# A decoder layer in split float32: the sums of a pair of down-projection blocks given one by one, a plain row block moved ahead of the second pair, and the up units split in one piece

## The chip, the cores and the metric

The kernel runs on one core of a Trainium2 chip. The core has five engines with a queue each: PE (TensorE, matmuls, with PEld for its weight loads), DVE (VectorE), ACT (ScalarE), POOL (GpSimd) and SP (SyncE, which here issues most DMAs). Each works through its own queue in order, and they wait for each other by semaphores. The metric is the device time of one execution in microseconds (us), lower being better. Before the change it is 417.64 us, the median of three runs (417.42 to 418.87).

## What is computed

One layer of a hybrid decoder, 256 tokens of 1024 channels, in float32. The change touches only the feed-forward part, the last third of the time:

```python
x = layer_norm(ALPHA * x + merged @ w_out[i], ln1_g[i], ln1_b[i])
h = jnp.square(jax.nn.relu(x @ w_up[i])) @ w_down[i]
ple = jax.nn.sigmoid(x @ w_ple_gate[i]) * (p[i] @ w_ple[i])
x = layer_norm(ALPHA * x + h + ple, ln2_g[i], ln2_b[i])
```

`w_up` is 1024 x 4096 and `w_down` 4096 x 1024.

## The kernel before

**Split operands.** PE takes float32 operands in a rounded form (F32R). To keep precision, each operand is split in a high part, rounded, and a low part, the rest. A product is three matmuls: high by high, high by low, low by high (`prod`, line 183). A weight unit is one [128, 1024] block. `Weights._split` gives its instructions: the DMA into `raw` (L102, from SP), the high part `whi` on ACT (L111, or L109 where the block is cut), and the low part `wlo` = raw - whi on DVE (L118, or L122). `whi` and `wlo` have five buffers each, so a unit's ACT instruction waits until PE has finished the unit five places back. `W.get(u)` returns a unit and gives out splits up to four units ahead (AHEAD). `W.subs` lists the last low-part instruction of every unit given so far.

**Up product.** 32 units, `f` from 0 to 31 (L922 on). Each takes eight 512-column matmuls with whi (L932) and eight 256-column ones with wlo (L935); DVE then sums the result out of PSUM (L916), ACT applies relu and square (L917, L918), and the result is split in turn. With the table `UP` (L639) the 128-column blocks of whi and wlo don't lie in one run: block 0 stands apart from the other seven (whi at 16 and then 192 to 1088, wlo at 64 and then 208 to 1104). The class `Apart` turns that into two instructions for each part, 256 and 768 columns wide in the profile.

**Down product.** The 32 row blocks of `w_down` are taken in the order of `SEQ` (L860), then 26 to 31 (`LATE`). A plain row block is one unit and 12 matmuls of 512 columns. A *pair* of row blocks is multiplied by a scheme of the Strassen kind: seven products of half blocks, 21 matmuls, for four units. For those, sums of the weights are formed on DVE first. `load(i)` fetches the two row blocks of pair i, three DMAs on SP (L885, L887 twice), into the buffer `xr` (two in turn). `form(i)` makes three sums: L894, 1024 wide, into `rows` (odd pairs) or `Y` (even); L895, 512 wide, into the loaded block itself; L896, 512 wide. The pair's units are then, in order: the second row block as loaded (unit 0), the first sum (unit 1), the first row block with the second sum in it (unit 2), the third sum, 512 wide (unit 3). Unit 0's raw is the loaded block; L118 rows read `wlo<-xr`, `wlo<-rows` or `wlo<-Y` for a pair's units and `wlo<-raw` for a plain block.

**What sets the order.** A scheduler with priorities places instructions on each engine's queue, by and large in the order in which the program gives them. Pair 0, blocks (0, 1), is loaded and formed in the up loop. Pairs 1 and 2, (4, 5) and (8, 9), are loaded and formed before the down product starts (L964). From then on, when unit 3 of pair i has been split, `last_part` puts pair i + 2 on the list `later`, and `weights` loads and forms it at once, all three sums in a row. The accumulators are the PSUM banks `P[1]` to `P[8]`; behind the last pair, `plus` (L1006) adds them up on DVE while PE multiplies blocks 24 and 25.

Of the kernel before, what the change touches and what calls it, by code (L numbers as in the profile page):

```python
# [13 lines left out]
ALU = mybir.AluOpType  # L14
# [128 lines left out]
def hybrid_layer(ctx: ExitStack, tc: tile.TileContext, x0, xn, pT, wqk, wva, wvb, wg, wbc, wba,  # L143
                 wout, wup, wdn, wpg, wple, lnrow, rel, onehot, pick, out):
    nc = tc.nc
    pe, act, dve, pool = nc.tensor, nc.scalar, nc.vector, nc.gpsimd
# [9 lines left out]
    W = Weights(tc, raw, part)  # L156
# [20 lines left out]
    t = banks.tile([128, 512], F32, name="b4", tag="b4")  # L177
# [54 lines left out]
    def add(*a, at=(0, 0), by=DV):  # L232
        i = n_u[0]
        n_u[0] += 1
        return W.add(*a, by=by if i < 58 else "v", at=at)
# [12 lines left out]
    for t in TASKS:  # L248
# [4 lines left out]
        elif t in "gcao":  # L253
            u, w, n = {"g": (u_g, wg, 1024), "c": (u_bc, wbc, 640), "a": (u_ba, wba, 768),
                       "o": (u_out, wout, 1024)}[t]
# [31 lines left out]
    def mmbank(shape):  # L287
        t = mm.tile([128, 512], F32, name="mm", tag="mm")
        return t[:, 0:256] if shape == 256 else t
# [89 lines left out]
    op = pm.tile([128, 8, 2, S], F32R, name="op")  # L379
# [159 lines left out]
    for j in range(4):  # L539
        s = s[2:] if j % 2 else logits(kI, iq[j], iq[j + 1])  # L540
        r = wk2.tile([128, 768], F32, name="ri", tag="eb")
        r = r.rearrange("p (h k) -> p h k", h=2)
        for h in range(2):
            act.activation(r[:, h], s[h], AF.Relu)
            n = 2 * j + h
# [42 lines left out]
    for j in range(3):  # L588
# [5 lines left out]
        for h in range(2):  # L594
            n = 2 * j + h
# [10 lines left out]
    for j in range(3):  # L606
        s = logits(kA, q)
        o = opair()
        for h in range(2):
            n = 2 * j + h  # L610
# [3 lines left out]
            with tc.issue_after(W.subs[-3]):  # L614
                pool.tensor_tensor(ta[:, 0:128], natural(T, n % 3, 128, 256), am[:, 0:128],
                                   op=ALU.add)
                pool.tensor_tensor(ta[:, 128:384], natural(T, n % 3, 0, 256), am[:, 128:384],
                                   op=ALU.add)
# [17 lines left out]
    u_out += [add(wout[4 + i], 1024, wo[:, i, 0], wo[:, i, 1]) for i in range(4)]  # L636
    u_ple = [add(wple[i], 1024) for i in range(2)]
    u_pg = [add(wpg[i], 1024) for i in range(8)]
    UP = (16, *range(192, 1088, 128)), (64, *range(208, 1104, 128))  # L639
    u_up = [[add(wup[i], 1024, at=UP)] for i in range(32)]  # L640

    H = (slice(0, 512), slice(512, 1024))
# [152 lines left out]
    for i in range(4):  # L795
# [4 lines left out]
        t = slice(b * 128, (b + 1) * 128)  # L800
# [51 lines left out]
    for b in range(2):  # L852
        for c in range(2):
# [3 lines left out]

    SEQ = ((0, 1), 2, 3, (4, 5), 6, 7, (8, 9), 10, (11, 12), 13, (14, 15), 16, (17, 18), 19,  # L860
           (20, 21), 22, 23, 24, 25)
    LATE = range(26, 32)
    PAIRS = [k for k in SEQ if isinstance(k, tuple)]
    hT, at, room = {}, 0, 0
    for k in (*SEQ, *LATE):
        i = PAIRS.index(k) if k in PAIRS else -1
        n = 512 if i < 0 else 1792
        if i in (0, 1):
            t = p2.tile([128, 2048], F32R, name=("X", "PL")[i], tag=("X", "PL")[i])[:, 0:n]
        elif i in (2, 3) or k == 2:  # L870
            t = more[:, room:room + n]
            room += n
        else:
            t = store[:, at:at + n]
# [4 lines left out]
    wr, wt = {}, {}  # L879

    def load(i):

        wr[i] = r = xr[:, i % 2] if i else p3.tile([128, 2, D], F32, name="rows", tag="rows")
        k1, k2 = PAIRS[i]
        nc.sync.dma_start(r[:, 0], wdn[k1])  # L885
        for h in range(2):
            nc.sync.dma_start(r[:, 1, H[h]], wdn[k2, :, H[1 - h]])  # L887

    def form(i):

        t = p3.tile([128, 2, D], F32, name="rows", tag="rows") if i % 2 else Y
        wt[i] = t = t.rearrange("p b d -> p (b d)")
        r = wr[i].rearrange("p b d -> p (b d)")
        dve.tensor_tensor(t[:, 0:1024], r[:, 512:1536], r[:, 0:1024], op=ALU.subtract)  # L894
        dve.tensor_tensor(r[:, 512:1024], r[:, 1024:1536], t[:, 0:512], op=ALU.subtract)  # L895
        dve.tensor_tensor(t[:, 1024:1536], r[:, 1536:2048], r[:, 512:1024], op=ALU.subtract)  # L896

    def last_part(i):
        r = wt[i][:, 1024:1536]
        if 0 < i < len(PAIRS) - 2:  # L900
            later.append(i + 2)
        return r

    later = []
    u_dn = {}
    for k in (*SEQ, *LATE):
        if k in PAIRS:
            i = PAIRS.index(k)
            u_dn[k] = [add(f, n) for f, n in (
                (lambda i=i: wr[i][:, 1], 1024), (lambda i=i: wt[i][:, 0:1024], 1024),  # L910
                (lambda i=i: wr[i][:, 0], 1024), (lambda i=i: last_part(i), 512))]
        elif k < 30:
            u_dn[k] = [add(wdn[k], 1024)]

    def relu2(dst, ps):
        dve.tensor_reduce(dst, ps.rearrange("p a t b -> p b t a"), axis=AX.X, op=ALU.add)  # L916
        act.activation(dst, dst, AF.Relu)  # L917
        act.activation(dst, dst, AF.Square)  # L918
# [3 lines left out]
    for f in range(32):  # L922
        if f == 16:
            with tc.issue_after(W.loads[-1]):
                load(0)
            with tc.issue_after(W.subs[-1]):
                form(0)
        ps = mmbank(512).rearrange("p (a t b) -> p a t b", a=2, b=2)
        hi, lo = W.get(u_up[f][0])
        cs = [slice(k * 128, (k + 1) * 128) for k in range(KT)]  # L930
        for k, c in enumerate(cs):
            pe.matmul(ps, lhsT=hi[:, c], rhs=x1[:, :, k].rearrange("p b a t -> p a t b"),  # L932
                      start=k == 0, stop=False)
        for k, c in enumerate(cs):
            pe.matmul(ps[:, 0], lhsT=lo[:, c], rhs=x1[:, :, k, 0].rearrange("p b t -> p t b"),  # L935
                      start=False, stop=k == KT - 1)
        if f not in half_of:
            spare = f % 2 == 0
            q = (p3.tile([128, 2, 128], F32, name="q1", tag="q1") if spare else
                 w2.tile([128, 8, 128], F32, name="a8", tag="a8")[:, 0:2])  # L940
            relu2(q, ps)
            q = q.rearrange("p b t -> p (b t)")
            act.copy(hT[f][:, 0], q)
            dve.tensor_tensor(hT[f][:, 1], q, hT[f][:, 0].bitcast(F32), op=ALU.subtract)
            continue
        j = half_of[f].index(f)
        if j == 0:
            a8 = w2.tile([128, 8, 128], F32, name="a8", tag="a8")
        relu2(a8[:, 2 * j:2 * j + 2], ps)
        if j == 0:  # L950
            continue

        a21, a11, a22, a12, *sums = (a8[:, j] for j in range(8))
        pool.tensor_tensor(sums[0], a21, a22, op=ALU.add)
        pool.tensor_tensor(sums[1], sums[0], a11, op=ALU.subtract)
        pool.tensor_tensor(sums[2], a11, a21, op=ALU.subtract)  # L956
        pool.tensor_tensor(sums[3], a12, sums[1], op=ALU.subtract)
        h = hT[half_of[f]]
        q = a8[:, 1:8].rearrange("p j t -> p (j t)")
        act.copy(h[:, 0], q)  # L960
        dve.tensor_tensor(h[:, 1], q, h[:, 0].bitcast(F32), op=ALU.subtract)

    xr = p3.tile([128, 2, 2, D], F32, name="xr", tag="x1")
    for i in (1, 2):  # L964
        load(i)
        form(i)

# [6 lines left out]
        fresh.discard(i)  # L976

    def weights(u):
        w = W.get(u)
        while later:  # L980
            i = later.pop(0)
            load(i)
            form(i)
        return w

    def plain(k, w, ids, end=False):
# [6 lines left out]
    TERMS = ((2, 2, 1), (3, 6, 0)), ((7, 5, 1), (5, 3, 0)), ((1, 0, 0), (6, 4, 1)), ((4, 1, 0),)  # L993
    for k in SEQ[:-2]:
        if k not in PAIRS:
            plain(k, weights(u_dn[k][0]), (3, 2, 4, 8), k == 23)
            continue
        for u, terms in zip(u_dn[k], TERMS):
            hi, lo = weights(u)
            for i, a, c in terms:  # L1000
                a = slice(128 * a, 128 * a + 128)
                onto(i, (hT[k][:, 0, a], hT[k][:, 1, a]), (wide(hi, H[c]), wide(lo, H[c])),
                     k == PAIRS[-1] and i in (1, 5, 6, 7))
# [56 lines left out]
    for b in range(2):  # L1060
        t = slice(128 * b, 128 * b + 128)
# [114 lines left out]
```

## Time and profile before

| | |
|---|---|
| three runs, us | 417.42, 417.64, 418.87 |
| the profiled execution, us | 417.59 |
| its span, first to last instruction, us | 415.8 |
| PE busy, us (share of the span) | 404.6 (97%) |
| PEld busy | 374.1 (90%) |
| DVE busy | 348.3 (84%) |
| ACT busy | 277.4 (67%) |
| POOL busy | 121.6 (29%) |
| DMA, GB/s mean over the span | 201 |

Times in rows of the profile are microseconds from the span's start, unless marked ns. A row of the timeline gives start, duration, engine, line, operation, what is written and read, and how many such instructions are merged; a bracket behind it gives the idle time of the engine before it and what ended it. PE's matmuls are pipelined: the next starts while the last one is still under way, so its busy share says little, and the distance between starts is what counts. A tile's name stands without its number (`b` and `mm` are PSUM banks, `store`, `more`, `X` and `PL` hold the split activations).

### The profile page before, as it was taken

Reading aid. Unit: us, or ns where it says so; the run is one execution under the profiler, and the core shown is the slowest. Engines: PE = TensorE matmul, PEld = TensorE weight load, DVE = VectorE, ACT = ScalarE, POOL = GpSimd, SP = SyncE. Lnnn points to the kernel's source line nnn. Section 1 sums busy time; section 2 is a strip of 40 time slices with the busy share of each in tenths; the row PEclk is TensorE's granted clock in tenths of the full one; section 3 lists DMA queues with packets and bytes.
Section 4 is the critical chain, followed back from the end, with each engine's and each line's share of the span. In section 5 each row is a group of like instructions: output and inputs, shape, how many; then the busy total and the mean of one; then the engine's idle time right before and its main releaser. Section 6 shows DMA issues by size and latency. Waiting matters only on the chain.

```text
span 415.8 us, 7826 instructions
## 1 busy us (share of the span) xinstructions
PE 404.6 (97%) x2804; PEld 374.1 (90%) x2804; DVE 348.3 (84%) x650; ACT 277.4 (67%) x530; POOL 121.6 (29%) x128
## 2 busy tenths in 40 slices
PE   8999999999999999999999999999999999899993
PEld 7989999999999999999887889999999888688882
DVE  4868769897777789889978889999999797999856
ACT  5787476495798786867515668887889675558310
POOL 1579456175353657500000002433330000000001
PEclk9999999999999999999999999999999999999998
DMA  8796766567474408477981677695675377546502
GB/s 283 291 338 184 273 166 199 170 202 259 143 208 135 134 18 285 123 217 259 332 314 36 225 268 207 223 298 177 195 214 186 128 271 215 189 159 212 192 2 102
DMA packets 27964, 83.49 MB, mean 201 GB/s; under 512 B 3184, under 2 KB 6792, under 8 KB 27540
## 3 DMA queue, kind: packets, MB, share of 16 engines
q1 hardware_dynamic: 27360, 81.51, 60.3%
q10 hardware_dynamic: 468, 1.41, 0.9%
q8 instruction: 22, 0.36, 0.4%
q14 instruction: 18, 0.15, 0.1%
q0 software_dynamic: 96, 0.06, 0.0%
HBM read 81.88 MB, written 1.09 MB: 200 GB/s over the span
## 4 chain that ended last, share of the span: by engine, by line
PE 79%; DVE 9%; DMA 6%; ACT 2%; issue 2%; SPq 0%; POOL 0%; DVEq 0%; ACTq 0%
PE mm L188 34%; PE b L188 17%; PE mm L932 13%; PE mm L935 7%; DMA xr<-in_wdn_dram 3%; PE b L370 3%; DVE wlo L118 3%; PE b L522 2%; DVE wlo L122 2%; DMA G<-in_x_dram 1%; DMA pr<-in_pT_dram 1%; PE b L412 1%; ACT whi L111 1%; PE b L419 1%; DVE Y L894 1%
## 5 line engine op out<-in xcount | busy, mean ns | idle before, releaser
L111 ACT CAST whi<-raw 128x1024 fp32r<-128x1024 f32 (+3 forms) x92 | 89.5, 986 | 35.6 <-PE b L188 14.5
L122 DVE TENSOR_TENSOR wlo<-raw,whi 128x256 fp32r<-128x256 f32 (+3 forms) x118 | 94.7, 826 | 15.3 <-ACT whi L111 11.4
L188 PE MATMUL mm<-xh,whi 128*128 128x256 f32 x336 | 89.1, 278 | 0.0
L122 POOL TENSOR_TENSOR wlo<-raw,whi 128x384 fp32r<-128x384 f32 (+1 forms) x50 | 68.7, 1383 | 65.0 <-ACT whi L111 57.6
L188 PE MATMUL mm<-xl,whi 128*128 128x256 f32 x336 | 87.1, 277 | 0.0
L188 PE MATMUL mm<-xh,wlo 128*128 128x256 f32 x336 | 79.4, 278 | 0.0
L188 PEld LDWEIGHTS mm<-xh,whi 128*128 128x128 f32 x336 | 64.5, 192 | 0.9
L188 PEld LDWEIGHTS mm<-xl,whi 128*128 128x128 f32 x336 | 64.5, 192 | 0.2
L932 PE MATMUL mm<-x,whi 128*128 128x512 f32 x256 | 60.8, 380 | 0.0
L188 PEld LDWEIGHTS mm<-xh,wlo 128*128 128x128 f32 x336 | 58.7, 192 | 0.2
L188 PE MATMUL b<-whi,store 128*128 128x512 f32 x168 | 52.5, 380 | 0.3 <-DVE b L1006 0.3
L932 PEld LDWEIGHTS mm<-x,whi 128*128 128x128 f32 x256 | 46.1, 190 | 5.1
L118 DVE TENSOR_TENSOR wlo<-raw,whi 128x1024 fp32r<-128x1024 f32 (+2 forms) x38 | 43.2, 1156 | 3.5 <-ACT whi L111 3.4
L749 POOL TENSOR_TENSOR rs<-rs,half 128x1 f32<-128x1 f32 x4 | 2.7, 666 | 142.5 <-DVE rs L748 142.5
L109 ACT CAST whi<-raw 128x256 fp32r<-128x256 f32 x64 | 36.4, 613 | 6.1 <-PE b L188 3.7
L188 PEld LDWEIGHTS b<-whi,store 128*128 128x128 f32 x168 | 31.8, 189 | 4.9 <-DVE b L1006 0.7
L935 PEld LDWEIGHTS mm<-x,wlo 128*128 128x128 f32 x256 | 33.6, 191 | 1.7
L935 PE MATMUL mm<-x,wlo 128*128 128x256 f32 x256 | 33.8, 275 | 0.0
L188 PE MATMUL b<-wlo,store 128*128 128x512 f32 x84 | 32.1, 382 | 0.6 <-DVE wlo L118 0.6
L956 POOL TENSOR_TENSOR a<-a 128x128 f32<-128x128 f32 x7 | 7.3, 1042 | 57.3 <-ACT a L918 51.7
L188 PE MATMUL mm<-op,whi 128*128 128x256 f32 x128 | 22.1, 278 | 0.0
L188 PE MATMUL b<-whi,x 128*128 128x512 f32 x64 | 19.8, 384 | 0.1
(221 smaller groups left out, 818.9 us busy)
## 6 DMA issues: line engine op xcount, KB each, us to landing
raw<-in_wup_dram SPq DMA_DIRECT2D x32, 512.0 KB, 4.4
raw<-in_wg_dram SPq DMA_DIRECT2D x24, 512.0 KB, 4.6
raw<-in_wqk_dram SPq DMA_DIRECT2D x18, 512.0 KB, 5.0
raw<-in_wdn_dram SPq DMA_DIRECT2D x18, 512.0 KB, 4.3
raw<-in_wout_dram SPq DMA_DIRECT2D x8, 512.0 KB, 4.5
raw<-in_wpg_dram SPq DMA_DIRECT2D x8, 512.0 KB, 5.2
T<-tabd SPq DMA_DIRECT2D x24, 128.0 KB, 4.0
xr<-in_wdn_dram SPq DMA_DIRECT2D x6, 512.0 KB, 3.6
```

What stands on the lines that cost most here:

```text
L109: i = nc.scalar.copy(blocks(hi, a, b), blocks(r, a, b))
L111: i = nc.scalar.copy(hi, r)
L118: i = e.tensor_tensor(lo[:, x], r[:, x], hi[:, x].bitcast(F32), op=ALU.subtract)
L122: i = e.tensor_tensor(blocks(lo, *x), blocks(r, *x), blocks(hi, *x).bitcast(F32), op=ALU.subtract)
L188: i = pe.matmul(ps, lhsT=a[x], rhs=b[y], start=first and n == 0, stop=last and n == 2, skip_group_check=more)
L370: m = pe.matmul(ss[2 * n + h][:, QC[b]], lhsT=q[d, x, c], rhs=k[d, y, 0:128 * (b + 1)], start=i == 0, stop=i == 2)
L412: pe.transpose(t[:, 128 * i:128 * i + 128], P[:, 128 * i:128 * i + 128], ident)
L419: pe.matmul(v[:, 256 * i:].rearrange("p (m c q) -> p m c q", c=64, q=2), lhsT=V[:, i, vh], rhs=pt[:, b0:b1].rearrange("p b a (q c) -> p (b ...
L522: pe.matmul(pairs(first[f]), lhsT=w[:, k, 128 * f:128 * f + 128], rhs=inturn(x[:, k]), start=k == i == 0, stop=k == KT - 1 and i == 2)
L932: pe.matmul(ps, lhsT=hi[:, c], rhs=x1[:, :, k].rearrange("p b a t -> p a t b"), start=k == 0, stop=False)
L935: pe.matmul(ps[:, 0], lhsT=lo[:, c], rhs=x1[:, :, k, 0].rearrange("p b t -> p t b"), start=False, stop=k == KT - 1)
L956: pool.tensor_tensor(sums[2], a11, a21, op=ALU.subtract)
```

## The change

There are three edits. The up units lie in one run, whi from column 64 and wlo from 80, so that each part is one instruction; blocks 1 to 7 stay at their columns, and block 0 moves (whi from 16 to 64, wlo from 64 to 80). Plain block 6 comes ahead of the pair (4, 5). And `form` becomes a generator that gives one sum at each call: the three sums of pair i are given behind the splits of units 1, 2 and 3 of pair i - 1, those of pair 1 behind the plain blocks 2, 3 and 6, each after that unit's last low-part instruction. Pair 0 and the loads are given as before.

```diff
-    UP = (16, *range(192, 1088, 128)), (64, *range(208, 1104, 128))
+    UP = 64, 80
...
-    SEQ = ((0, 1), 2, 3, (4, 5), 6, 7, (8, 9), 10, (11, 12), 13, (14, 15), 16, (17, 18), 19,
+    SEQ = ((0, 1), 2, 3, 6, (4, 5), 7, (8, 9), 10, (11, 12), 13, (14, 15), 16, (17, 18), 19,
...
-        dve.tensor_tensor(t[:, 0:1024], r[:, 512:1536], r[:, 0:1024], op=ALU.subtract)
-        dve.tensor_tensor(r[:, 512:1024], r[:, 1024:1536], t[:, 0:512], op=ALU.subtract)
-        dve.tensor_tensor(t[:, 1024:1536], r[:, 1536:2048], r[:, 512:1024], op=ALU.subtract)
+        yield dve.tensor_tensor(t[:, 0:1024], r[:, 512:1536], r[:, 0:1024], op=ALU.subtract)
+        yield dve.tensor_tensor(r[:, 512:1024], r[:, 1024:1536], t[:, 0:512], op=ALU.subtract)
+        yield dve.tensor_tensor(t[:, 1024:1536], r[:, 1536:2048], r[:, 512:1024],
+                                op=ALU.subtract)
...
+    for i in range(1, len(PAIRS)):
+        behind = u_dn[PAIRS[i - 1]][1:] if i > 1 else u_dn[2] + u_dn[3] + u_dn[6]
+        for n, u in enumerate(behind):
+            steps[u] = i, n
+    going = {}
...
     for i in (1, 2):
         load(i)
-        form(i)
...
     def weights(u):
+        n = W.done
         w = W.get(u)
         while later:
-            i = later.pop(0)
-            load(i)
-            form(i)
+            load(later.pop(0))
+        for n in range(n, W.done):
+            if n in steps:
+                with tc.issue_after(W.subs[n]):
+                    next(going.setdefault(steps[n][0], form(steps[n][0])))
         return w
```

How that moves DVE's queue is seen at three places. First, between plain block 10 and plain block 13, where pair 3, (11, 12), is split and pair 4, (14, 15), is formed. Pair 3's sums lie in `rows`, pair 4's in `Y`. Before:

```order
L118 TENSOR_TENSOR wlo<-raw,whi 128x1024
L894 TENSOR_TENSOR Y<-xr 128x1024
L118 TENSOR_TENSOR wlo<-xr,whi 128x1024
L118 TENSOR_TENSOR wlo<-rows,whi 128x1024
L895 TENSOR_TENSOR xr<-xr,Y 128x512
L118 TENSOR_TENSOR wlo<-xr,whi 128x1024
L118 TENSOR_TENSOR wlo<-rows,whi 128x512
L896 TENSOR_TENSOR Y<-xr 128x512
L118 TENSOR_TENSOR wlo<-raw,whi 128x1024
```

and now:

```order
L118 TENSOR_TENSOR wlo<-raw,whi 128x1024
L896 TENSOR_TENSOR rows<-xr 128x512
L118 TENSOR_TENSOR wlo<-xr,whi 128x1024
L118 TENSOR_TENSOR wlo<-rows,whi 128x1024
L894 TENSOR_TENSOR Y<-xr 128x1024
L118 TENSOR_TENSOR wlo<-xr,whi 128x1024
L118 TENSOR_TENSOR wlo<-rows,whi 128x512
L895 TENSOR_TENSOR xr<-xr,Y 128x512
L118 TENSOR_TENSOR wlo<-raw,whi 128x1024
L896 TENSOR_TENSOR Y<-xr 128x512
```

Pair 4's first sum stood ahead of all four splits of pair 3 and now stands behind two of them; its second sum moves behind the other two, and its third behind plain block 13.

Second, DVE's first sums of the down product, pairs 1 and 2 (pair 1 in `rows`, pair 2 in `Y`). Before:

```order
L894 TENSOR_TENSOR rows<-xr 128x1024
L118 TENSOR_TENSOR wlo<-xr,whi 128x1024
L895 TENSOR_TENSOR xr<-xr,rows 128x512
L894 TENSOR_TENSOR Y<-xr 128x1024
L118 TENSOR_TENSOR wlo<-rows,whi 128x1024
```

and now:

```order
L894 TENSOR_TENSOR rows<-xr 128x1024
L118 TENSOR_TENSOR wlo<-raw,whi 128x1024
L118 TENSOR_TENSOR wlo<-xr,whi 128x1024
L895 TENSOR_TENSOR xr<-xr,rows 128x512
L118 TENSOR_TENSOR wlo<-rows,whi 128x1024
L894 TENSOR_TENSOR Y<-xr 128x1024
```

The split of plain block 6 now stands between pair 1's first sum and its first split, and pair 2's first sum moves behind pair 1's unit 1.

Third, DVE in the up loop, behind the split of the activations of pair 0. Before:

```order
L961 TENSOR_TENSOR X<-a_3543,X 128x896
L944 TENSOR_TENSOR more<-q_3606,more 128x256
L122 TENSOR_TENSOR wlo<-raw,whi 128x2x128
L122 TENSOR_TENSOR wlo<-raw,whi 128x768
L916 TENSOR_REDUCE a_3668<-mm 128x256
```

and now (the same code stands five or six lines further down in the changed file):

```order
L967 TENSOR_TENSOR X<-a_3533,X 128x896
L950 TENSOR_TENSOR more<-q_3592,more 128x256
L921 TENSOR_REDUCE a_3650<-mm 128x256
L118 TENSOR_TENSOR wlo<-raw,whi 128x1024
```

A unit's low part is one instruction instead of two, and so is its high part on ACT.

More of the change, by code (lines that the diff above doesn't have):

```diff
@@ L893, in form @@
         r = wr[i].rearrange("p b d -> p (b d)")
-        dve.tensor_tensor(t[:, 0:1024], r[:, 512:1536], r[:, 0:1024], op=ALU.subtract)
-        dve.tensor_tensor(r[:, 512:1024], r[:, 1024:1536], t[:, 0:512], op=ALU.subtract)
-        dve.tensor_tensor(t[:, 1024:1536], r[:, 1536:2048], r[:, 512:1024], op=ALU.subtract)
+        yield dve.tensor_tensor(t[:, 0:1024], r[:, 512:1536], r[:, 0:1024], op=ALU.subtract)
+        yield dve.tensor_tensor(r[:, 512:1024], r[:, 1024:1536], t[:, 0:512], op=ALU.subtract)
+        yield dve.tensor_tensor(t[:, 1024:1536], r[:, 1536:2048], r[:, 512:1024],
+                                op=ALU.subtract)
     def last_part(i):
-        r = wt[i][:, 1024:1536]
         if 0 < i < len(PAIRS) - 2:
             later.append(i + 2)
-        return r
+        return wt[i][:, 1024:1536]
     later = []
-    u_dn = {}
+    u_dn, steps = {}, {}
     for k in (*SEQ, *LATE):
@@ L926, in hybrid_layer @@
             with tc.issue_after(W.subs[-1]):
-                form(0)
+                for _ in form(0):
+                    pass
         ps = mmbank(512).rearrange("p (a t b) -> p a t b", a=2, b=2)
```

## The prediction

> **What bounds the kernel now.** I read the busy times by stage first, then the matmuls' start times, then what the late ones waited for. A row of the stage view gives the stretch, its length, then busy time and count of PE, PEld, DVE, ACT and POOL, the granted clock, the DMA share and GB/s. The six stretches are the up product, three parts of the down product's first 267 matmuls, the extra sums, and the end.
>
> ```profile
> core 0: us, PE busy (x) PEld busy (x) DVE busy (x) ACT busy (x) POOL busy (x), PEclk, DMA share, GB/s
> 244.00:327.28 83.28, 83.28 (x511) 76.55 (x510) 80.17 (x126) 70.05 (x149) 21.47 (x28) 1.00 0.65 198
> 327.28:354.50 27.22, 27.22 (x129) 23.80 (x128) 23.20 (x26) 16.75 (x21) 0.00 (x0) 1.00 0.75 245
> 354.50:361.40 6.90, 5.75 (x24) 4.02 (x23) 6.90 (x9) 4.16 (x5) 0.00 (x0) 1.00 0.49 166
> 361.40:381.50 20.10, 20.09 (x93) 17.30 (x92) 20.03 (x22) 12.23 (x14) 0.00 (x0) 1.00 0.55 186
> 381.50:390.50 9.00, 8.74 (x41) 7.33 (x41) 8.96 (x11) 5.39 (x7) 0.00 (x0) 1.00 0.78 254
> 390.50:415.80 25.30, 18.21 (x102) 16.29 (x100) 14.70 (x26) 3.41 (x4) 1.82 (x3) 0.94 0.15 56
> ```
>
> PE is never idle in the up product. Its only gaps before the end lie at 354.5 to 361.4 and near 390, and there DVE is busy throughout. Matmuls overlap in these rows, so I measure a loss by start times. The floor comes from the up product (start, duration, instruction, count):
>
> ```profile
> 251.30 1.89 PE L932 MATMUL mm<-x,whi 128*128 128x512 f32 x8
> 253.03 1.05 PE L935 MATMUL mm<-x,wlo 128*128 128x256 f32 x8
> 253.92 0.81 PE L932 MATMUL mm<-x,whi 128*128 128x512 f32 x3
> ```
>
> Eight 512-column matmuls take 253.03 - 251.30 = 1.73 us: one every 0.216 us; eight of 256 columns take 0.89, one every 0.111. What exceeds 0.216 per matmul in the down product is lost. These are all the places where that is over 0.06 us, behind the stage's first matmul (the bracket names idle time and its releaser):
>
> ```profile
> 327.28 0.38 PE L188 MATMUL b<-whi,X 128*128 128x512 f32 x1
> ...
> 354.48 0.81 PE L188 MATMUL mm<-whi,more 128*128 128x512 f32 x3
> 355.89 0.48 PE L188 MATMUL b<-wlo,more 128*128 128x512 f32 x1 [0.59 <-DVE wlo L118]
> 356.21 0.38 PE L188 MATMUL b<-whi,more 128*128 128x512 f32 x1
> ...
> 357.99 0.81 PE L188 MATMUL b<-whi,store 128*128 128x512 f32 x3
> 358.76 0.48 PE L188 MATMUL mm<-wlo,more 128*128 128x512 f32 x1
> 359.08 0.38 PE L188 MATMUL mm<-whi,more 128*128 128x512 f32 x1
> ...
> 360.16 0.38 PE L188 MATMUL b<-whi,store 128*128 128x512 f32 x1
> 361.10 0.48 PE L188 MATMUL b<-wlo,store 128*128 128x512 f32 x1 [0.56 <-DVE wlo L118]
> 361.42 0.38 PE L188 MATMUL b<-whi,store 128*128 128x512 f32 x1
> ...
> 375.01 0.59 PE L188 MATMUL b<-whi,store 128*128 128x512 f32 x2
> 375.62 0.48 PE L188 MATMUL b<-wlo,store 128*128 128x512 f32 x1
> 375.94 0.38 PE L188 MATMUL b<-whi,store 128*128 128x512 f32 x1
> ...
> 389.54 0.38 PE L188 MATMUL b<-whi,store 128*128 128x512 f32 x1
> 390.18 0.48 PE L188 MATMUL b<-whi,store 128*128 128x512 f32 x1 [0.26 <-DVE b L1006]
> 390.50 0.38 PE L188 MATMUL b<-wlo,store 128*128 128x512 f32 x1
> ```
>
> At 354.48 three matmuls should end 0.65 later, at 355.13; the next starts at 355.89, so 0.76 is lost, and the matmul after a wait starts 0.32 behind it, 0.10 more. By the same sums: 0.12 + 0.10 at 358.76, 0.72 + 0.10 at 361.10, 0.18 + 0.10 at 375.62, 0.42 + 0.10 at 390.18. That is **1.90 us** around pair 3, **0.28** at 375 and **0.52** at 390. Each of the first four waits for a wlo, DVE's subtraction. Why is DVE late?
>
> ```profile
> 332.17 1.23 DVE L894 TENSOR_TENSOR rows<-xr 128x1024 f32<-128x1024 f32 x1 [0.57 <-DMA xr<-in_wdn_dram]
> ...
> 350.12 0.68 DVE L896 TENSOR_TENSOR rows<-xr 128x512 f32<-128x512 f32 x1
> 350.73 1.22 DVE L118 TENSOR_TENSOR wlo<-raw,whi 128x1024 fp32r<-128x1024 f32 x1
> 353.47 1.23 DVE L894 TENSOR_TENSOR Y<-xr 128x1024 f32<-128x1024 f32 x1 [1.53 <-DMA xr<-in_wdn_dram]
> 354.61 1.22 DVE L118 TENSOR_TENSOR wlo<-xr,whi 128x1024 fp32r<-128x1024 f32 x1
> ```
>
> At the queue's head stands the first sum of pair 4 (L894), whose rows have not landed; the four splits of pair 3 stand behind it, and the first of them is the wlo that PE awaits at 355.89. DVE idles 1.53 us and then works without a gap to 390, still late for units 13 and 19. Its pace: a 1024-wide instruction every 1.14 us (354.61 - 353.47), a 512-wide one every 0.60 (350.73 - 350.12). The load of pair 4 itself:
>
> ```profile
> 349.03 0.33 SPq L885 DMA_DIRECT2D xr<-in_wdn_dram  x1
> ```
>
> It is issued when pair 2's third split has ended, and its sum starts 353.47 - 349.03 = 4.44 us later.
>
> **The change, part by part.**
>
> *Sums given singly.* No instruction is added; 18 move on DVE (pairs 1 to 6, three each). From the third split of pair i-2, which lets the load of pair i go, the queue before held sum 0.60, split 0.60, sum 0.60, split 1.14 = 2.94 us ahead of pair i's first sum, against 4.44 for the load: 1.5 us idle, as the bracket says. Now it holds 0.60 + 0.60 + 1.14 + 0.60 and two splits of the next pair, 2 x 1.14: 5.2 us. The load is covered with 0.8 to spare, and the two splits that PE needs first no longer stand behind it. The loads on SP keep their order, apart from one raw load that now stands ahead of pair 3's.
>
> *Row block 6 ahead of pair 1.* PE gets 12 matmuls, 2.59 us, before it needs pair 1, and DVE a split to do where it idled after 332.17. Does DVE keep ahead? From 332.17 to the end of unit 7's split there are 7 long and 5 short instructions: 332.17 + 7.98 + 3.00 = 343.15. PE starts the down product at 327.28 and meets unit 7 after 78 matmuls (two pairs of 21, three row blocks of 12): 344.13, a lead of 1.0. To unit 10 DVE takes 6.9 and PE 33 x 0.216 = 7.13; then each round costs DVE five long and three short, 7.50, against 7.13. The lead is 1.2 at unit 10, 0.84 at 13, 0.47 at 16, 0.10 at 19. A row block opens with three matmuls on whi (the x3 at 357.99), so its wlo is wanted 0.65 later still: the thinnest cover is **0.75 us**, at unit 19. After it no more sums are formed. ACT hides its splits: it is busy 16.75 of 27.22 us. So the 1.90 and the 0.28 go; if a cover fails, what is short is paid once, at units 16 to 19.
>
> *The end of the pairs.* The 0.52 at 390.18 waits for DVE's additions (L1006):
>
> ```profile
> 383.50 0.68 DVE L1006 TENSOR_TENSOR Y<-mm,Y 128x512 f32<-128x512 f32 x1
> ...
> 389.43 0.69 DVE L1006 TENSOR_TENSOR b<-b,Y 128x512 f32<-128x512 f32 x1
> ...
> 380.89 1.05 ACT L111 CAST whi<-raw 128x1024 fp32r<-128x1024 f32 x1 [0.46 <-PE mm L188]
> ...
> 382.32 0.59 ACT L1013 COPY Y<-mm 128x512 f32<-128x512 f32 x1
> ```
>
> Before, the first was free to run when ACT's copy ended, 382.91, and started at 383.50 because DVE was still on splits. With PE 2.18 earlier the copy ends at 380.73; unit 24's whi, which PE releases (380.89), then its wlo on DVE end at 378.71 + 1.05 + 1.14 = 380.90. From there the addition that PE needs starts 389.43 - 383.50 = 5.93 later and takes 0.69: 387.52. PE is there at 389.54 + 0.22 - 2.18 = 387.58. The wait goes by a hair; I count 0.45 of 0.52, with 0 and 0.52 as ends.
>
> *Up units in one piece.* For each unit ACT and DVE lose one instruction of two. On DVE (mean ns after the busy time, over the up product):
>
> ```profile
> L122 DVE TENSOR_TENSOR wlo<-raw,whi 128x768 fp32r<-128x768 f32 x28 | 28.1, 1003 | 0.0
> L122 DVE TENSOR_TENSOR wlo<-raw,whi 128x256 fp32r<-128x256 f32 x28 | 12.3, 441 | 0.0
> ```
>
> Two pieces take 1.44 us, one 1.22 (354.61): at most 0.22 less, 6.2 us over 28 units. But PE is busy 83.28 of 83.28 us in this stage, so it is worth nothing. But block 0 of whi and wlo moves to another column, which no row of this kernel shows for L932 and L935. The price lies between 0 and the 0.10 that a matmul loses when its weights are not loaded ahead (356.21 - 355.89 against 0.216). The nearest row: a transpose, whose weights lie in quite another tile, behind a 256-column matmul.
>
> ```profile
> 89.03 0.28 PE L188 MATMUL mm<-xl,whi 128*128 128x256 f32 x1
> 89.14 0.27 PE L412 MATMUL b<-ident,eb 128*128 128x128 f32 x1
> ```
>
> It follows 0.11 us behind, the pace of the L935 rows. I take 0.
>
> The Trainium skill, "SBUF — State Buffer", section "SBUF: two separate sides", says that on the engines' side only the port pair shared by VectorE and GpSimd is contended and that PE never waits on another's access. By that the price is 0; the row at 89.14 agrees.
>
> **Sum.** 1.90 + 0.28 + 0.45 = 2.63 us off 417.59, the profiled execution's own time (its span is 415.8; the median of the three runs, 417.64, is the same within 0.05): **415.0 us**. With nothing from the end it is 415.4, with all of it 414.9.
>
> **The rivals.**
> - *Block 0's new place costs weight loads* (the slower side). 64 loads move. At 0.10 each that is 6.4 us, less 2.63: 421.4. If only the 32 behind a 256-column matmul suffer, 3.2: 418.2. It beats the gain from 2.63 / 32 = 82 ns per unit. For it: a matmul every 0.111 us leaves a load little room. Against: the row at 89.14. Chance 0.09.
> - *The wait for the load only moves.* The sums have 5.2 us; the loads took 4.44 here, but with 6 us each of pairs 4 to 6 loses 0.8, 2.4 in all, against a cover of 0.75: 1.65 back, 416.6. For it: DVE is the busiest engine and loses 0.37 of its lead each round. Against: three loads of this size at once took no longer than that. Chance 0.14.
> - *PE is not at its floor in the up product, DVE is*: then up to 6.2 us of one-piece splits would show: 408.8. For it: DVE is busy 80.17 of 83.28 us. Against: PE waits for nothing there. Chance 0.02.
>
> The Trainium skill, "TensorE: Matmul & The Clock Gate", section "Back-to-back issue gap", gives some 131 ns per 512-column matmul in a stream of weight loads and matmuls, by which PE would have room here. Every one stands 216 ns from the next, so the trace does not bear it out.
>
> **How the numbers follow.** Forecast 0.73 (414.5 to 415.5). The range runs from 414.4, all of the 2.7 and the measurement's scatter, to 417.0, which takes in the moved wait; the dear layout is left out above, some 0.1. Half a per cent, 2.1 us, is what a measurement of this kernel can tell from no change: faster needs 415.5 or less. That holds the forecast but for a rest, and the third rival: 0.72. Within: the moved wait, the half-dear layout: 0.22. Slower: the full price of the layout, 0.06.
>
> **What would show it.** Right: no PE gap over 0.1 us from 327 to 385; L894 of pairs 3 to 6 without a DMA releaser; DVE's idle time after 332 only behind unit 23; the up product still 2.62 us per unit. Wrong: brackets "<-DVE wlo" at units 13 to 19, a DMA bracket at L894, or the up product longer than 83.3 us (then block 0's place costs).

## The result, and the profile after

| | median us | lowest to highest | executions |
|---|---|---|---|
| before | 417.43 | 417.03 to 418.87 | 6 |
| after | 414.94 | 414.27 to 415.49 | 6 |

The ratio is 0.9936, with a 95% interval from 0.9919 to 0.9953: 2.5 us less. The profiled execution of after took 415.19 us (span 413.4), against 417.59 (415.8) before.

The same stage view of the kernel after, with the columns that the prediction explains:

```profile
244.00:327.28 83.28, 83.28 (x512) 76.48 (x511) 76.36 (x96) 66.30 (x118) 20.68 (x28) 1.00 0.64 199
327.28:354.50 27.22, 27.22 (x129) 23.84 (x128) 25.55 (x29) 18.03 (x23) 0.00 (x0) 1.00 0.77 255
354.50:361.40 6.90, 6.90 (x34) 6.04 (x33) 6.90 (x9) 4.61 (x6) 0.00 (x0) 1.00 0.69 211
361.40:381.50 20.10, 20.10 (x95) 17.55 (x94) 20.10 (x22) 14.22 (x17) 0.00 (x0) 1.00 0.52 176
381.50:390.50 9.00, 8.76 (x41) 7.37 (x40) 8.97 (x13) 3.14 (x4) 0.00 (x0) 1.00 0.75 252
```

The third row is the one to read: PE was busy 5.75 of these 6.90 us before, and 6.90 now. In the up product PE is busy throughout as before, 83.28 of 83.28. The fifth row still has a gap. It is the only one between 327 and 412, shown here by the matmuls' starts:

```profile
327.27 0.38 PE L188 MATMUL b<-whi,X 128*128 128x512 f32 x1
...
387.28 0.38 PE L188 MATMUL b<-whi,store 128*128 128x512 f32 x1
387.89 0.48 PE L188 MATMUL b<-whi,store 128*128 128x512 f32 x1 [0.24 <-DVE b L1014]
388.21 0.38 PE L188 MATMUL b<-wlo,store 128*128 128x512 f32 x1
```

387.89 - 387.28 - 0.216 = 0.39 is lost there (0.40 before rounding), and 0.10 by the matmul after it: 0.50 us, still for an addition (L1006 is L1014 now). The down product begins at 327.27 as before. From there to the end it took 415.8 - 327.28 = 88.5 us before and 413.4 - 327.27 = 86.1 now. So all 2.4 us lie behind the start of the down product. 2.70 - 0.50 = 2.20 of them are PE's waits; the other 0.2 lie in steps too small to be counted here and behind the down product's last matmul.

The first sums of pairs 3 and 4 on DVE with what stands beside them, and the loads of these pairs on SP's queue:

```profile
344.88 1.22 DVE L118 TENSOR_TENSOR wlo<-Y,whi 128x1024 fp32r<-128x1024 f32 x1
346.13 1.23 DVE L894 TENSOR_TENSOR rows<-xr 128x1024 f32<-128x1024 f32 x1
...
353.62 1.22 DVE L894 TENSOR_TENSOR Y<-xr 128x1024 f32<-128x1024 f32 x1
354.76 1.22 DVE L118 TENSOR_TENSOR wlo<-xr,whi 128x1024 fp32r<-128x1024 f32 x1
```

```profile
340.92 0.33 SPq L885 DMA_DIRECT2D xr<-in_wdn_dram  x1
...
348.52 0.33 SPq L885 DMA_DIRECT2D xr<-in_wdn_dram  x1
```

No bracket names a DMA any more, here or at the sums of pairs 5 and 6. Pair 4's sum stands 353.62 - 348.52 = 5.1 us behind its load and does not wait; before, it stood 4.44 us behind it, 1.53 of them waiting.

### The profile page after: what moved, and what is told of

The parts are those of the page before. It is cut to its first block, busy times and chain, and to the rows that moved or that the text cites. A ratio compares the mean times of both kernels' runs of the same rounds, so it can differ in the third digit from the quotient of the medians.

```text
span 413.4 us, 7773 instructions
## 1 busy us (share of the span) xinstructions
PE 403.5 (98%) x2804; PEld 374.5 (91%) x2804; DVE 344.9 (83%) x618; ACT 275.0 (67%) x498; POOL 120.7 (29%) x128
## 4 chain that ended last, share of the span: by engine, by line
PE 78%; DVE 12%; DMA 5%; issue 3%; POOL 1%; ACT 0%; SPq 0%; DVEq 0%; POOLq 0%
PE mm L188 35%; PE b L188 14%; PE mm L938 13%; PE mm L941 7%; DVE wlo L118 6%; PE b L370 3%; PE b L522 3%; DMA xr<-in_wdn_dram 2%; DMA pr<-in_pT_dram 1%; PE b L412 1%; PE b L419 1%; DVE wlo L122 1%; DMA raw<-in_wdn_dram 1%; DVE Y L894 1%; DVE xr L895 1%
## 5 line engine op out<-in xcount | busy, mean ns | idle before, releaser
L111 ACT CAST whi<-raw 128x1024 fp32r<-128x1024 f32 (+3 forms) x124 | 122.6, 1000 | 39.5 <-PE b L188 15.6
L188 PE MATMUL mm<-xh,whi 128*128 128x256 f32 x336 | 89.1, 278 | 0.0
L118 DVE TENSOR_TENSOR wlo<-raw,whi 128x1024 fp32r<-128x1024 f32 (+2 forms) x70 | 82.8, 1195 | 5.8 <-ACT whi L111 5.6
L188 PE MATMUL mm<-xl,whi 128*128 128x256 f32 x336 | 87.1, 277 | 0.0
L188 PE MATMUL mm<-xh,wlo 128*128 128x256 f32 x336 | 79.4, 278 | 0.0
L188 PEld LDWEIGHTS mm<-xh,whi 128*128 128x128 f32 x336 | 64.4, 192 | 0.9
L188 PEld LDWEIGHTS mm<-xl,whi 128*128 128x128 f32 x336 | 64.5, 192 | 0.2
L122 DVE TENSOR_TENSOR wlo<-raw,whi 128x640 fp32r<-128x640 f32 (+2 forms) x54 | 51.4, 959 | 13.2 <-ACT whi L111 11.7
L188 PEld LDWEIGHTS mm<-xh,wlo 128*128 128x128 f32 x336 | 58.7, 192 | 0.2
L188 PE MATMUL b<-whi,store 128*128 128x512 f32 x168 | 52.4, 380 | 0.2 <-DVE b L1014 0.2
L188 PEld LDWEIGHTS b<-whi,store 128*128 128x128 f32 x168 | 31.8, 189 | 5.0 <-DVE b L1014 0.6
L941 PEld LDWEIGHTS mm<-x,wlo 128*128 128x128 f32 x256 | 33.5, 191 | 1.7
L941 PE MATMUL mm<-x,wlo 128*128 128x256 f32 x256 | 33.8, 275 | 0.0
L188 PE MATMUL b<-wlo,store 128*128 128x512 f32 x84 | 31.8, 379 | 0.0
L188 PE MATMUL mm<-op,whi 128*128 128x256 f32 x128 | 22.1, 278 | 0.0
L962 POOL TENSOR_TENSOR a<-a 128x128 f32<-128x128 f32 x7 | 3.9, 563 | 54.6 <-ACT a L923 54.6
L188 PE MATMUL b<-whi,x 128*128 128x512 f32 x64 | 19.8, 384 | 0.1
L188 PEld LDWEIGHTS mm<-op,whi 128*128 128x128 f32 x128 | 18.8, 192 | 0.3
```

Source lines behind the costliest of these rows:

```text
L111: i = nc.scalar.copy(hi, r)
L118: i = e.tensor_tensor(lo[:, x], r[:, x], hi[:, x].bitcast(F32), op=ALU.subtract)
L122: i = e.tensor_tensor(blocks(lo, *x), blocks(r, *x), blocks(hi, *x).bitcast(F32), op=ALU.subtract)
L188: i = pe.matmul(ps, lhsT=a[x], rhs=b[y], start=first and n == 0, stop=last and n == 2, skip_group_check=more)
```

## The experiments

Before, after and the eleven further runs in one table. "Loss" is worked out as in the prediction: for every matmul that starts over 0.06 us late from 327 to 412, what its distance to the one ahead has over 0.216, added up. The start of the down product is the first L188 matmul behind the up product, and "from there to the end" is the span less that start, both in the run's one profile. Each ratio is to the runs of before that were made with it (medians 417.43, 417.37, 416.99 and 417.20).

| kernel | median us | ratio to before, 95% interval | start of the down product | from there to the end | loss |
|---|---|---|---|---|---|
| before | 417.43 | | 327.28 | 88.5 | 2.70 |
| after | 414.94 | 0.9936 (0.9919 to 0.9953) | 327.27 | 86.1 | 0.50 |
| up units alone | 417.52 | 1.0005 (0.9995 to 1.0015) | 327.75 | 88.0 | 2.30 |
| sums and block 6, no up units | 414.66 | 0.9938 (0.9922 to 0.9953) | 327.08 | 85.7 | 0.10 |
| block 6 alone | 417.10 | 0.9989 (0.9977 to 1.0000) | 327.29 | 88.7 | 3.03 |
| sums alone, with up units | 415.04 | 0.9942 (0.9926 to 0.9957) | 327.97 | 86.2 | 0.53 |
| wlo columns from 64 | 414.36 (one) | | 326.81 | 85.8 | 0.10 |
| addition ahead | 415.03 | 0.9955 (0.9941 to 0.9969) | 327.98 | 85.6 | 0 |
| sums one split earlier | 416.12 | 0.9979 (0.9968 to 0.9990) | 327.25 | 87.2 | 1.54 |
| addition ahead, up units as before | 414.32 | 0.9937 (0.9925 to 0.9949) | 327.20 | 85.6 | 0 |
| after, again | 415.06 | 0.9950 (0.9935 to 0.9965) | 327.66 | 85.7 | 0.17 |
| addition ahead, again | 414.81 | 0.9946 (0.9926 to 0.9965) | 327.41 | 85.6 | 0 |
| both, again | 414.83 | 0.9949 (0.9931 to 0.9968) | 328.26 | 85.6 | 0 |

Two columns carry the argument. The time from the down product's start to the end, less the loss, is 85.6 to 85.8 in every row: the waits of PE explain all of it but 0.2 us. And the start itself wanders from 326.81 to 328.26, also for one kernel (327.27 and 327.66 for after). So half a microsecond is read from the traces, not from the medians.

**The parts of the change, one by one.** First the up units alone:

```diff
 # before, with
-    UP = (16, *range(192, 1088, 128)), (64, *range(208, 1104, 128))
+    UP = 64, 80
```

> The kernel before with the up units in one piece, nothing else. Theory (PE is at its floor in the up product, block 0's new place costs nothing): the up product keeps 83.28 us, 2.62 per unit; DVE's work there falls from 80.2 to some 76 us without use, and DVE comes into the down product some 0.6 us later than before (its first sum at 332.8 instead of 332.2), which the wait for whi behind that sum (0.47 us) swallows but for 0.1. Time 417.4, within 0.3 of before. Rival 'the split in one piece brings the gain': the whole 2.5 us show here, 415. Rival 'the new place costs weight loads': up product longer by 3.2 or 6.4 us, 420.6 or 423.8.

It is no faster. The up product keeps its pace. The stage view of this kernel:

```profile
244.00:327.28 83.28, 83.28 (x509) 76.42 (x508) 76.30 (x97) 66.25 (x117) 20.65 (x28) 1.00 0.63 201
...
354.50:361.40 6.90, 6.34 (x27) 4.59 (x26) 6.90 (x9) 4.62 (x5) 0.00 (x0) 1.00 0.52 169
```

DVE works 76.30 us instead of 80.17 in the first row, PE 83.28 as ever, and the gap of the third row is still there, 0.56 instead of 1.15. DVE does come later, as expected: it forms its first sum 333.05 - 327.75 = 5.30 us behind the start of the down product, 332.17 - 327.28 = 4.89 before. The smaller loss, 2.30 against 2.70, is no gain: PE entered the down product 0.47 us later in this execution, and the matmul that waits at 361.10 starts at 361.10 in both.

Then the change without that edit (after, with the old UP):

```diff
 # after, with
-    UP = 64, 80
+    UP = (16, *range(192, 1088, 128)), (64, *range(208, 1104, 128))
```

> The change without its edit to the up units. Theory: the 1.90 + 0.28 us come from the sums, so they stay, with no matmul gap over 0.1 us from 327 to 385. Beyond that, if DVE's late entry after the change (first sum at 332.78 against 332.17 before) comes from the up units in one piece, the first sum stands at 332.2 here, the additions at the end come 0.6 us earlier, and the last wait falls from 0.50 to under 0.1: 414.5. Rival 'DVE enters late for another reason': first sum at 332.8, wait of 0.5 at the end, 414.9. Rival 'the gain is the up units' ': 417.4.

The whole gain is there, and the last wait is 0.10. Its first sum and the split of block 19 on DVE, and the matmul that needs this split:

```profile
332.00 1.23 DVE L894 TENSOR_TENSOR rows<-xr 128x1024 f32<-128x1024 f32 x1 [0.59 <-DMA xr<-in_wdn_dram]
...
371.17 1.22 DVE L118 TENSOR_TENSOR wlo<-raw,whi 128x1024 fp32r<-128x1024 f32 x1
```

```profile
372.85 0.59 PE L188 MATMUL b<-whi,store 128*128 128x512 f32 x2
373.28 0.38 PE L188 MATMUL b<-wlo,store 128*128 128x512 f32 x1
```

The split ends at 371.17 + 1.14 = 372.31, 0.97 us ahead of its matmul.

Block 6 alone:

```diff
 # before, with
-    SEQ = ((0, 1), 2, 3, (4, 5), 6, 7, ...
+    SEQ = ((0, 1), 2, 3, 6, (4, 5), 7, ...
```

> The kernel before with row block 6 ahead of pair 1, sums given as before. Theory (what counts is how many splits stand between a pair's load and its first sum): the sums of pairs 3 and 4 still find their rows not landed, with DMA brackets of 0.5 to 1.8 us at the first sums, and PE stalls of some 2 us from unit 10 or 13 on; at most 0.6 us are won: 416.8 to 417.4. Rival 'the lead that block 6 gives is what counts': most of the gain, 415.3.

0.3 us in the median, and no less loss in the trace. The first sums of pairs 3 and 4 on DVE, and the first place where PE pays:

```profile
346.15 1.23 DVE L894 TENSOR_TENSOR rows<-xr 128x1024 f32<-128x1024 f32 x1 [2.65 <-issue]
...
355.04 1.23 DVE L894 TENSOR_TENSOR Y<-xr 128x1024 f32<-128x1024 f32 x1 [0.18 <-DMA xr<-in_wdn_dram]
```

```profile
347.36 0.38 PE L188 MATMUL mm<-whi,more 128*128 128x512 f32 x1
348.57 0.48 PE L188 MATMUL b<-wlo,more 128*128 128x512 f32 x1 [0.83 <-DVE wlo L118]
```

The wait has only moved, from pair 4's sum to pair 3's. The bracket of the 2.65 us names no DMA, but the rows were still on their way: the last issue of pair 3's load stands at 340.58, 5.57 us ahead of the sum, and the trace has 5.5 us from it to the landing.

The sums alone (with the up units in one piece, block 6 in its old place):

```diff
 # after, with
-    SEQ = ((0, 1), 2, 3, 6, (4, 5), 7, ...
+    SEQ = ((0, 1), 2, 3, (4, 5), 6, 7, ...
...
-        behind = u_dn[PAIRS[i - 1]][1:] if i > 1 else u_dn[2] + u_dn[3] + u_dn[6]
+        behind = u_dn[PAIRS[i - 1]][1:] if i > 1 else u_dn[2] + u_dn[3] + u_dn[4, 5][:1]
```

> The change with block 6 in its old place behind pair 1; pair 1's sums stand behind blocks 2 and 3 and its own first unit. Theory: no DMA bracket over 0.2 us at the first sums of pairs 3 to 6, and nearly all of the gain. DVE idles some 0.5 us behind its first sum, where block 6's split stood, and since after the change the wlo of unit 19 came with no time left (its split ended at 373.21, PE wanted it at 373.2), those 0.5 us show as a PE wait at unit 16 or 19 (wlo): 415.4, between 415.2 and 415.8. Rival 'block 6 is needed for the lead': waits of over 1 us in all at units 10 to 19, 416.3 or more. Rival 'the cover of 0.75 us holds': no wait for wlo, 414.9.

Nearly all of the gain, with 0.53 lost and that only at the end. The wait at block 16 or 19, and with it the 415.2 to 415.8, did not come: DVE was idle 0.20 us where I had worked out 0.5. The rival that the cover holds did come.

```profile
333.26 1.22 DVE L894 TENSOR_TENSOR rows<-xr 128x1024 f32<-128x1024 f32 x1
334.68 1.23 DVE L118 TENSOR_TENSOR wlo<-xr,whi 128x1024 fp32r<-128x1024 f32 x1 [0.20 <-ACT whi L111]
...
381.99 0.68 DVE L1014 TENSOR_TENSOR Y<-mm,Y 128x512 f32<-128x512 f32 x1
```

So the order of the sums is nearly the whole gain: it takes 2.17 of the 2.70 us away. What block 6 adds is small, and it shows only where DVE enters the down product at the same time. Here DVE's first sum stands 333.26 - 327.97 = 5.29 us behind PE's start and its first addition 381.99 - 327.97 = 54.02. In the second profile of the kernel after (shown below) it is 5.30 and 53.61. So block 6 brings DVE 0.4 us forward, and PE's last wait falls from 0.53 to 0.17. Against the first profile of after, where the first sum came 0.2 us later, only 0.03 of that is left, and the medians (415.04 against 414.94 and 415.06) do not show it.

**The column of block 0.** A third place for wlo's columns:

```diff
 # after, with
-    UP = 64, 80
+    UP = 64, 64
```

> The change with wlo's columns beginning at 64 instead of 80, so that block 0 and all others stand elsewhere once more. Theory (a column costs no weight load anything): the up product 2.62 us per unit, 83.3 us, and a matmul of L941 every 0.111 us as before. Rival 'the column counts': pitch of L941 or of the first L938 of a unit over 0.111, up product longer by 3 us or more.

The up product of this kernel, stage view and matmuls:

```profile
244.00:327.28 83.28, 83.28 (x511) 76.49 (x511) 76.01 (x96) 66.29 (x119) 20.69 (x28) 1.00 0.64 197
```

```profile
252.55 1.05 PE L941 MATMUL mm<-x,wlo 128*128 128x256 f32 x8
253.44 1.89 PE L938 MATMUL mm<-x,whi 128*128 128x512 f32 x8
255.17 1.05 PE L941 MATMUL mm<-x,wlo 128*128 128x256 f32 x8
```

From one L941 row to the next it is 2.62 us, and eight of its matmuls take 253.44 - 252.55 = 0.89, in the third layout as in the first two.

**How much queued work the load needs.** The sums one split earlier:

```diff
 # after, with
-        behind = u_dn[PAIRS[i - 1]][1:] if i > 1 else u_dn[2] + u_dn[3] + u_dn[6]
+        behind = u_dn[PAIRS[i - 1]][:3] if i > 1 else u_dn[2] + u_dn[3] + u_dn[6]
```

> The change with every sum of pairs 2 to 6 one split earlier in DVE's queue: the first behind one split of the pair ahead instead of two. The load then has 3.48 us of queued work ahead of its sum (0.60 + 0.60 + 1.14 + 1.14) instead of 5.2; loads took 3.5 to 4.4 us in the kernel before. Theory (the queued work in front of the first sum is what hides the load): pair 3's sum reaches the head at 344.9 and waits for its rows until 346.1, 1.1 us more than after the change, the sums of pairs 4 to 6 wait 0 to 0.95 us each, with a DMA named in the bracket; since the wlo of unit 19 has 0.2 us to spare after the change, nearly all of it reaches PE: 1.0 to 4 us, so 416 to 419. Rival 'the sums' place counts only against pair 3's own splits, the load is hidden anyway': no DMA bracket over 0.2 us, 414.9.

It is 1.2 us slower than after by the medians, 1.8 by the ratios to before: 1.04 more loss, nearly all of it spread over PE's waits from 350 to 375. The first sums of pairs 3 and 4, and the loads of pairs 3 and 4:

```profile
345.77 1.23 DVE L894 TENSOR_TENSOR rows<-xr 128x1024 f32<-128x1024 f32 x1 [1.02 <-issue]
...
353.53 1.22 DVE L894 TENSOR_TENSOR Y<-xr 128x1024 f32<-128x1024 f32 x1 [0.18 <-DMA xr<-in_wdn_dram]
```

```profile
340.71 0.33 SPq L885 DMA_DIRECT2D xr<-in_wdn_dram  x1
...
349.90 0.33 SPq L885 DMA_DIRECT2D xr<-in_wdn_dram  x1
```

DVE idles 1.02 + 0.18 = 1.20 us; what reaches PE is 1.04. It is the lower end of what I had set: pair 4's sum started 353.53 - 349.90 = 3.63 us behind its load here, not 4.44. Pair 3's started 345.77 - 340.71 = 5.06 behind its own and paid nearly all of the idle time. Its bracket names no DMA, but the trace has the landings: 5.0 us behind the issue for pair 3, 3.5 for pair 4.

**The last wait.** The addition ahead of two splits, which needs those splits to be given later:

```diff
-    def weights(u):
+    def weights(u, ahead=AHEAD):
         n = W.done
-        w = W.get(u)
+        w = W.get(u, ahead)
...
-            plain(k, weights(u_dn[k][0]), (3, 2, 4, 8), k == 23)
+            plain(k, weights(u_dn[k][0], {22: 3, 23: 2}.get(k, AHEAD)), (3, 2, 4, 8), k == 23)
...
-        dve.tensor_tensor(o, a, b, op=ALU.add)
+        return dve.tensor_tensor(o, a, b, op=ALU.add)
...
-    plus(P[4], P[4], v3)
+    W.after = (plus(P[4], P[4], v3).ins,)
```

> The change with the addition that PE waits for at the end of the pairs ahead of the splits of row blocks 26 and 27 (2.3 us of DVE work) instead of behind them. Theory: the 0.50 us at 387.9 are owed to DVE's place in its queue alone, so the wait goes and nothing else moves, since those splits are needed several us later: no matmul gap over 0.1 us from 327 to 410, profiled loss 0.50 smaller, 414.5 against 414.9. Rival 'PE's end is set by something behind it (the later splits, the last loads)': a wait of the same size at 390 to 395, 414.9.

The same with the line UP of before, that is with the up units in two pieces:

> The addition ahead of the two splits, and the up units in two pieces as before (DVE enters the down product 0.6 us earlier). Theory: PE has nothing left to wait for between 327 and 410 in either, so this is no faster than the addition alone: 414.4 to 414.6; wlo of unit 19 has 0.9 us to spare instead of 0.2. Rival 'both gains add up': 414.1.

The addition starts at 385.38 and the splits follow it, so no loss is left, and the stretch to the end is 85.6 us in both. DVE's queue in the first of the two:

```profile
385.38 0.70 DVE L1014 TENSOR_TENSOR b<-b,Y 128x512 f32<-128x512 f32 x1
385.98 2.35 DVE L118 TENSOR_TENSOR wlo<-raw,whi 128x1024 fp32r<-128x1024 f32 x2
```

Yet the first's median was 415.03, where 414.5 was expected, and the second's 414.32, between what was expected and its rival. So both ran once more beside the kernel after:

> The changed kernel once more, for its last wait. In its first profile the wait for the addition was 0.50 us; the same order with other columns showed 0.10. Theory: which it is is decided in each execution by when DVE forms its first sum (5.51 us after PE's start of the down product in the first profile, 5.29 in the other): with 5.3 the addition starts 53.6 us after PE's start and the wait is 0.1, with 5.5 it is 0.5. Rival 'columns': 5.5 and 0.5 again whatever. Time 414.4 to 415.0.

> The addition ahead of the two splits, once more beside the changed kernel on the same chip. Theory: no wait at 387 in any execution, from PE's start of the down product to the end 85.6 us; the 415.03 of the first time came from what lies ahead of the down product, which started 0.7 us later in that profile than in that of the change and is not of this edit. Time 0 to 0.5 us below the changed kernel of this call. Rival 'the edit costs something ahead of the down product': its start again at 328.0 and a time not below the changed kernel's.

> The addition ahead and the up units in two pieces, beside the changed kernel on the same chip. Theory: 85.6 us from PE's start of the down product to the end, at most 0.5 us below the changed kernel: 414.3 against 414.4 to 415.0.

The kernel after lost only 0.17 us at its end this time. DVE in that profile:

```profile
332.62 0.42 DVE L950 TENSOR_TENSOR store<-a,store 128x256 fp32r<-128x256 f32 x1
332.96 1.22 DVE L894 TENSOR_TENSOR rows<-xr 128x1024 f32<-128x1024 f32 x1
...
381.27 0.68 DVE L1014 TENSOR_TENSOR Y<-mm,Y 128x512 f32<-128x512 f32 x1
```

The first sum stands 332.96 - 327.66 = 5.30 us behind PE's start, the first addition 53.61. In the first profile of after it was 332.78 - 327.27 = 5.51 and, from 381.22, 53.95. So the size of the wait depends on the execution, as expected, and not on the columns. The addition put ahead takes it away in all four profiles. In time that is 414.81 and 414.83 against 415.06: about as large as the traces say, and too small for the medians to settle. The 414.3 expected of the last one did not come; its down product started at 328.26, the latest of all.

## Why the prediction was right, step by step

- **PE is at its floor in the up product, the split in one piece is worth nothing: right.** DVE's splits of this stage are 28 of 1239 ns now:

```profile
L118 DVE TENSOR_TENSOR wlo<-raw,whi 128x1024 fp32r<-128x1024 f32 x28 | 34.7, 1239 | 0.1
```

By the records, 28.1 + 12.3 - 34.7 = 5.7 us went. But one record overlaps the next by 0.08 (1.22 us at a pace of 1.14), so the queue gained less than that: DVE's busy time in the first row of the stage view fell by 80.17 - 76.36 = 3.8, and the 6.2 that the prediction set as the most was too much. PE gained none of it. DVE did not even come earlier. What DVE waited for from 244 to 327, after and then before (us in total, times, longest):

```profile
DVE more L967 <- ACT more L966: 2.6, 2, 1.3
DVE PL L967 <- ACT PL L966: 1.3, 1, 1.3
DVE store L967 <- ACT store L966: 1.3, 1, 1.3
...
```

```profile
...
DVE more L961 <- ACT more L960: 0.4, 2, 0.2
...
```

The saved time turned into waits for ACT at the pairs' stores (L967, the line L961 of before): 5.2 us instead of 0.4, and the same 5.2 with the up units alone.
- **Block 0's new place costs nothing: right.** Three layouts, one pace: 83.28 us busy of 83.28 in each. The Trainium skill, "SBUF — State Buffer", section "SBUF: two separate sides", says that PE never waits on another engine's access, and these rows agree. The sentence speaks of other engines and not of columns; that the column costs nothing is what the three layouts show.
- **The 1.90 and the 0.28 go because the sums no longer stand ahead of their rows: right.** The sums alone take them away, block 6 or the up units alone do not, and one split less ahead of the sums brings 1.04 of loss back.
- **The load is covered with 0.8 to spare: too simple.** I took 4.44 us for every load, from one row. The profile of before already had a longer one, at pair 3:

```profile
344.37 1.23 DVE L894 TENSOR_TENSOR rows<-xr 128x1024 f32<-128x1024 f32 x1 [0.59 <-DMA xr<-in_wdn_dram]
```

Its load's last issue stands at 339.73, 4.64 us ahead. And pair 2's three issues, right behind pair 1's, took 5.7 to 6.4 us each to land, so the argument against that rival, that three such loads at once took no longer, is not borne out there. After the change pair 3's sum stood 346.13 - 340.92 = 5.21 behind its load, with 346.13 - 344.88 - 1.14 = 0.11 of idle time ahead of it, where a cover of 5.2 had been reckoned: the load took 5.1 us to land. In the second execution it took 4.5, and the sum did not wait. So pair 3 had between nothing and some 0.5 us to spare, and pair 4, whose load took 3.7, had 1.4. Pair 3's load now has one more raw load ahead of it on SP; that this made it longer was not tried by itself.
- **DVE's lead, with 0.75 us to spare at block 19: right where DVE enters as I assumed, thinner in the change.** I began the sum at DVE's old entry, 332.17. With that entry (the run without the up units) 0.97 was left. In the kernel after, these are the split and its matmul:

```profile
372.07 1.22 DVE L118 TENSOR_TENSOR wlo<-raw,whi 128x1024 fp32r<-128x1024 f32 x1
```

```profile
373.03 0.59 PE L188 MATMUL b<-whi,store 128*128 128x512 f32 x2
373.46 0.38 PE L188 MATMUL b<-wlo,store 128*128 128x512 f32 x1
```

373.46 - 372.07 - 1.14 = 0.25. In the second execution it is 373.85 - 372.12 - 1.14 = 0.59. Block 6, which was to give the lead, gives 0.4 us of it; the sums alone kept ahead of PE's wlo without it.
- **0.45 of the 0.52 at the end: this is the term that was mis-sized.** 0.02 came in the first profile of after (0.50 left) and 0.35 in the second (0.17 left). The chain was right: from the first addition to the one that PE needs it is 387.15 - 381.22 = 5.93 us, as I had it, and where DVE has room the first addition starts 53.6 us behind PE's start, which is my 380.90 (380.90 - 327.28 = 53.62). What failed is "DVE has room": the up units in one piece, which I had put down as worth nothing, make DVE ready later. Before, it was done with the up product at 331.19 + 0.34 and waited 0.57 us for rows:

```profile
331.19 0.42 DVE L944 TENSOR_TENSOR store<-a,store 128x256 fp32r<-128x256 f32 x1
332.17 1.23 DVE L894 TENSOR_TENSOR rows<-xr 128x1024 f32<-128x1024 f32 x1 [0.57 <-DMA xr<-in_wdn_dram]
```

In the first profile of after:

```profile
332.22 0.42 DVE L950 TENSOR_TENSOR store<-a,store 128x256 fp32r<-128x256 f32 x1
332.78 1.22 DVE L894 TENSOR_TENSOR rows<-xr 128x1024 f32<-128x1024 f32 x1
...
377.81 3.49 DVE L118 TENSOR_TENSOR wlo<-raw,whi 128x1024 fp32r<-128x1024 f32 x3
381.22 0.68 DVE L1014 TENSOR_TENSOR Y<-mm,Y 128x512 f32<-128x512 f32 x1
...
387.15 0.69 DVE L1014 TENSOR_TENSOR b<-b,Y 128x512 f32<-128x512 f32 x1
```

It is done 1.03 us later, the first sum slips by 0.61, and the three splits run into the additions without a gap. Two things decide when the first sum comes. One is when DVE is done with the up product: 4.24 us behind PE's start in all five profiles with the up units in two pieces, 5.29 to 5.34 in all eight with one piece. The other is when pair 1's rows land. With two pieces DVE waited for them every time, and the sum stood between 4.89 and 5.27; with one piece it stood at DVE's 5.29 to 5.34 seven times, and the last wait was 0.10 and 0.17 in the two of these that have the order of the kernel after (wlo columns from 64, and the second profile of after).

Only in the first profile of after did the rows come later still. The sum needs L885's rows and those of the first L887. That L887, issued at 327.85, took 4.8 us to land, against 4.4 in the second profile and 4.2 in that of before. So DVE was done at 332.22 + 0.34 = 332.56 and formed the sum at 332.78; in the second profile it formed it at once (332.62 + 0.34 = 332.96). No bracket names this wait, but the landing accounts for it. With the 0.11 at pair 3's sum these 0.2 us turned the wait of 0.17 into 0.50. I had called it "by a hair", and a hair it is. Whether the shorter splits make DVE late, or their new place in its queue behind L921, was not tried apart.

The sum came out at 415.0 against 414.94 and 415.06. That it fits to 0.1 is partly luck: PE's waits shrank by 2.20 us in the first profile, not by 2.63, 0.2 came from outside them, and the start of the down product scatters by more than that. Of the rivals, none happened. The nearest was the wait for the load that only moves: it took block 6 without the sums, or the sums one split earlier, to see it.

## What to carry to other kernels

- Where an in-order engine forms something from a load, count the work queued between the load's issue and its first use against the longest such load in the trace, not against one row. Moving the use behind other work of the same engine cost nothing here.
- Work saved on an engine that isn't the bound can still move that engine. Here giving each split as one piece took 3.8 us off DVE's busy time, and DVE came a microsecond later into the next stage; the term of the sum that started from its old entry was the one that went wrong.
- A gain "by a hair" should stand in the sum as a toss between nothing and all, and not near its better end.

## What the runs showed of the hardware

- One and the same kind of load (two row blocks of w_down in three issues) took 3.5 us for pair 4 and 5.0 for pair 3 in one execution (the sums one split earlier), from the issue of L885 to its landing; pair 3's took 5.1 and 4.5 in two executions of the kernel after. So a single row of such a load is no price for the others, nor for itself in the next execution.
- The start of the down product wandered by 1.45 us (326.81 to 328.26) between single executions, while what followed it, less PE's waits, was equal within 0.2 us. From the up product's first matmul to that start it is 83.84 us in all eight profiles with the up units in one piece, and 88.16 or 88.17 in all five with two, where two matmuls of the first unit stand ahead of the end of the product before. So this scatter lies ahead of the up product, in a part that the change doesn't reach.
